# A two-block fp32 network whose residual stream is kept by token, not by channel

## The chip, the cores and the metric

One core of a Trainium2 chip runs the whole program. The metric is the device time of one execution in microseconds (us). The engines named below are TensorE (PE, matrix products; PEld is its weight load), VectorE (DVE), ScalarE (ACT), GpSimd (POOL) and SyncE (SP, which here only starts transfers).

## What is computed

A sequence of 256 tokens with 2048 channels goes through two blocks. In block 1 the residual stream h takes up a mixer (a gated recurrence beside a sparse attention), an MLP of width 8192 with a squared ReLU, and a gate fed by an embedding p of each layer. In block 2 it takes up a second mixer, a SwiGLU FFN of width 5632, a state-space mixer (s5) and another FFN. Around each part stand norms:

```python
def rms_norm(x, g):
    xf = x.astype(jnp.float32)
    y = xf * lax.rsqrt(jnp.mean(xf * xf, axis=-1, keepdims=True) + NORM_EPS)
    return (y * g.astype(jnp.float32)).astype(x.dtype)
...
h = h + rms_norm(part(rms_norm(h, gain_pre)), gain_post)
```

The last line is the pattern of a part, in short form; in the gate it is `h = h + sigmoid(h @ W_gate) * (p @ W_proj)` without norms. All of it is fp32.

## The kernel before, in words

Products are made from rounded halves: an operand x is split into x_hi (rounded, made by ACT, L245 or L248) and x_lo (the rest, made by DVE, L246 or L249); a weight chunk that was loaded as wr is split into wh (ACT, L261) and wl (DVE, L262). Each product of a weight tile is then three passes of PE: wh with x_hi and x_lo, and wl with x_hi. A chunk holds two k (a k is 128 channels of the contraction) by 512 columns, and four chunks of wh and wl are held, so that the next wh can be written once PE has ended a chunk.

`group` (L304) leaves its result by channel (128 channels on the partitions, 256 tokens along the row); `atok` (L786 to L788) leaves it by token (128 tokens on the partitions, two halves c, columns along the row). The output products of a part use `outs`, which is `atok` over column groups of 512 and, at the very end, two of 256.

h is a tile of 16 k by 256 tokens, by channel, and so is the operand X of the next product. The output Y of a part is by token, where the norm's factor r is a number for each partition. `post_norm` turns and scales at once: for each k and token half it multiplies Y by a 128x128 diagonal matrix `dg` of r on PE (L577, fp32, which the records show as two), and DVE adds the result with the gain (a number for each channel, thus for each partition) to h (L578). `make_x` calls this `upd(k)` ahead of the split of each k, so the first column group of a part runs as: update k, split k, multiply by k. Sums of squares of h, for the next norm, are one ACT square and two products with a column of ones for each k (`h_norm`, L540 and L542); r itself comes from an integer guess and three Newton steps in small DVE operations (`rsqrt_small`, L402 to L410). For s5 the squares are summed by products with a matrix of ones (L1862).

```python
        dg = [self.s([P, P], tag="dg", bufs=2) for _ in range(2)]
        for c in range(2):
            V.tensor_scalar(dg[c], self.ident, r[:, c:c + 1], None, op0=ALU.mult)
...
            for c in range(2):
                nc.tensor.matmul(pt[:, c * P:(c + 1) * P], Y[:, c, k * P:(k + 1) * P], dg[c], start=True, stop=True)
            V.scalar_tensor_tensor(self.h[:, k], pt, self.vec(gain[0], gain[1] + k), self.h[:, k], op0=ALU.mult, op1=ALU.add)
```

Each engine runs its own queue in order; a scheduler lays the queues out by priorities while the program is built. Weight loads, and what else is loaded on SP, are issued in the order of SP's queue as their buffers come free. The seams between parts are, in order: the start, mixer to MLP, MLP to gate, gate to mixer 2, mixer 2 to the first FFN, FFN to s5, s5 to the second FFN, and the end.

## Time and profile before

| | us |
|---|---|
| median of three runs (3611.12 to 3624.04) | 3619.83 |
| the profiled execution | 3617.48 |
| its span | 3615.7 |
| PE busy in it | 3485.3 |
| DVE busy | 2152.0 |
| ACT busy | 1737.1 |
| POOL busy | 904.5 |

The granted clock of PE had a mean of 0.983 of its full rate. PE is busy nearly all the time, so what matters is read from the chain that ended last: where PE's own instructions follow each other it is PE's work that sets the time, and where another engine stands in the chain PE waits for it. A busy time of PE counts overlapping instructions whole; the chain counts only what each adds.

### The profile page before, as it was taken

The page shows a single profiled execution, that of the slowest core. Times are in us where ns is not written, and L with a number is a line of the kernel's source. Part 1 is how long each engine was busy: PE and PEld are TensorE (multiplying, and loading weights), DVE is VectorE, ACT ScalarE, POOL GpSimd, SP SyncE. Part 2 cuts the span into 40 slices and gives each one's busy share as a digit, 9 for nine tenths or more (in the row PEclk, how much of TensorE's full clock was granted, in tenths as well). Part 3 has the DMA queues.
Part 4 walks back from the last instruction along what each step waited for, and adds up shares of the span by engine and source line. Part 5 has one row for each costly group of instructions (what it writes and reads, how often), then busy time and mean ns, then how long its engine had stood idle before and what let it go on. Part 6 is the DMA issues. An engine that isn't in the chain of part 4 may idle for free.

```text
span 3615.7 us, 55161 instructions
## 1 busy us (share of the span) xinstructions
PE 3485.3 (96%) x20610; PEld 2998.3 (83%) x20610; DVE 2152.0 (60%) x3323; ACT 1737.1 (48%) x2621; POOL 904.5 (25%) x1378
## 2 busy tenths in 40 slices
PE   9989999998999999999899999999779999999999
PEld 9877788886888898998788888888668888888887
DVE  6687674555555656555666466565664565465565
ACT  4656554643344554445444444344454454444443
POOL 0231022288610002010436565644310000000000
PEclk9999999998999999999999999999989999999999
DMA  7735456676776564565567777778876466665664
GB/s 218 225 111 158 135 166 195 186 217 195 218 210 198 154 198 134 147 181 181 162 207 227 235 231 220 247 217 256 284 223 195 137 187 192 192 191 188 192 189 138
DMA packets 506148, 699.28 MB, mean 193 GB/s; under 512 B 43318, under 2 KB 317143, under 8 KB 505880
## 3 DMA queue, kind: packets, MB, share of 16 engines
q1 hardware_dynamic: 473712, 628.99, 57.1%
q0 software_dynamic: 27456, 63.65, 5.8%
q8 instruction: 161, 2.64, 0.3%
q10 hardware_dynamic: 4712, 3.13, 0.3%
q14 instruction: 107, 0.88, 0.1%
HBM read 654.17 MB, written 37.22 MB: 191 GB/s over the span
## 4 chain that ended last, share of the span: by engine, by line
PE 85%; POOL 5%; DVE 4%; DMA 3%; ACT 2%; issue 1%; SPq 0%; ACTq 0%; DVEq 0%; POOLq 0%
PE ps L304 34%; PE px L304 11%; PE ps L786 11%; PE ps L788 11%; PE ps L787 11%; POOL m L1737 1%; POOL m L1738 1%; POOL m L1739 1%; PE px L577 1%; PE pm L1756 1%; DMA TBd<-m 1%; DVE wl L262 1%; ACT wh L261 1%; PE pm L542 0%; DMA m<-in_wg_dram 0%
## 5 line engine op out<-in xcount | busy, mean ns | idle before, releaser
L262 DVE TENSOR_TENSOR wl<-wr,wh 128x1024 fp32r<-128x1024 f32 x1126 | 1427.9, 1269 | 1239.7 <-ACT wh L261 1199.1
L261 ACT ACTIVATE wh<-wr 128x1024 fp32r<-128x1024 f32 x1126 | 1190.4, 1058 | 1441.0 <-PE ps L788 538.4
L304 PE MATMUL ps<-x,wh 128*128 128x512 f32 (+1 forms) x4864 | 1285.9, 353 | 12.8 <-DVE e L381 4.6
L304 PE MATMUL ps<-x,wl 128*128 128x256 f32 x3840 | 856.5, 283 | 1.5 <-DVE wl L262 1.5
L304 PEld LDWEIGHTS ps<-x,wl 128*128 128x128 f32 x3840 | 729.5, 191 | 130.3 <-issue 5.5
L304 PEld LDWEIGHTS ps<-x,wh 128*128 128x128 f32 x4864 | 760.8, 192 | 29.0 <-issue 10.8
L786 PE MATMUL ps<-wh,x 128*128 128x512 f32 (+1 forms) x2032 | 768.4, 378 | 5.6 <-ACT wh L261 3.6
L787 PE MATMUL ps<-wl,x 128*128 128x512 f32 (+1 forms) x2032 | 762.7, 375 | 0.8 <-DVE wl L262 0.8
L788 PE MATMUL ps<-wh,x 128*128 128x512 f32 (+1 forms) x2032 | 762.3, 375 | 0.0
L786 PEld LDWEIGHTS ps<-wh,x 128*128 128x128 f32 x2032 | 383.1, 189 | 79.5 <-ACT wh L261 4.1
L788 PEld LDWEIGHTS ps<-wh,x 128*128 128x128 f32 x2032 | 383.1, 189 | 70.3 <-issue 2.0
L787 PEld LDWEIGHTS ps<-wl,x 128*128 128x128 f32 x2032 | 383.5, 189 | 69.0 <-issue 1.8
L304 PE MATMUL px<-x,wh 128*128 128x512 f32 x1280 | 404.9, 397 | 1.8 <-DVE e L381 1.8
L304 PEld LDWEIGHTS px<-x,wl 128*128 128x128 f32 x1280 | 240.1, 188 | 56.7 <-issue 0.8
L304 PE MATMUL px<-x,wl 128*128 128x256 f32 x1280 | 256.0, 280 | 0.3 <-DVE wl L262 0.3
L304 PEld LDWEIGHTS px<-x,wh 128*128 128x128 f32 x1280 | 196.7, 189 | 4.7 <-issue 2.0
L245 ACT ACTIVATE x<-e 128x256 fp32r<-128x256 f32 x168 | 68.3, 411 | 87.9 <-DVE e L1540 48.7
L1798 POOL TENSOR_TENSOR m<-m,m 128x128 f32<-128x128 f32 x128 | 68.7, 559 | 120.7 <-PE pm L1756 106.7
L577 PE MATMUL px<-dg,x 128*128 128x128 f32 x384 | 62.8, 309 | 29.7 <-DVE dg L568 28.7
L246 DVE TENSOR_TENSOR x<-e,x 128x256 fp32r<-128x256 f32 x168 | 79.3, 480 | 15.4 <-ACT x L245 12.5
L1815 POOL TENSOR_TENSOR m<-m,m 128x256 f32<-128x256 f32 x64 | 59.5, 933 | 102.2 <-DMA m<-in_s5bT_dram 102.2
L577 PEld LDWEIGHTS px<-dg,x 128*128 128x128 f32 x384 | 56.6, 216 | 33.7 <-DVE dg L568 21.0
(487 smaller groups left out, 2774.2 us busy)
## 6 DMA issues: line engine op xcount, KB each, us to landing
wr<-in_w_ffn_in_dram SPq DMA_DIRECT2D x704, 256.0 KB, 3.2
wr<-in_mlp_w_dram SPq DMA_DIRECT2D x256, 512.0 KB, 4.5
wr<-in_w_ffn_out_dram SPq DMA_DIRECT2D x176, 512.0 KB, 4.8
wr<-in_w_in_dram SPq DMA_DIRECT2D x152, 512.0 KB, 3.9
wr<-in_w_out_dram SPq DMA_DIRECT2D x64, 512.0 KB, 4.0
wr<-in_w_glu_dram SPq DMA_DIRECT2D x128, 256.0 KB, 3.1
wr<-in_ple_gate_dram SPq DMA_DIRECT2D x32, 512.0 KB, 4.7
wr<-in_w_in_dram SPq DMA_DIRECT2D x32, 256.0 KB, 5.8
```

Source lines behind the costliest of these rows:

```text
L245: a = nc.scalar.activation(dst[:, 0], src, AF.Copy)
L246: b = (eng or nc.vector).tensor_tensor(dst[:, 1], src, dst[:, 0].bitcast(F32), op=ALU.subtract)
L261: nc.scalar.activation(wh, wr, AF.Copy)
L262: nc.vector.tensor_tensor(wl, wr, wh.bitcast(F32), op=ALU.subtract)
L304: mm = lambda o, w, x, a, z: nc.tensor.matmul(o, w, x, start=a, stop=z, skip_group_check=True)
L577: nc.tensor.matmul(pt[:, c * P:(c + 1) * P], Y[:, c, k * P:(k + 1) * P], dg[c], start=True, stop=True)
L786: nc.tensor.matmul(ps, xh, wh, start=first, stop=False, skip_group_check=True)
L787: nc.tensor.matmul(ps, xh, wl, start=False, stop=False, skip_group_check=True)
L788: nc.tensor.matmul(ps, xl, wh, start=False, stop=last, skip_group_check=True)
L1737: G_.tensor_tensor(o, x[:, :, 0:n], c0, op=ALU.mult)
L1798: G_.tensor_tensor(t1[:, q], u_(1), l_(1), op=ALU.mult)
L1815: G_.tensor_tensor(ob[:, :, ri], v4(gb[0][:, 0]), v4(gb[1][:, ri]), op=ALU.mult)
```

## The change

h is kept by token, as Y is. The update is then a DVE operation with r as a number for each partition (`scalar_tensor_tensor`, for two k at once and each token half, in line L603 of the changed kernel), and PE turns each 128x128 tile of h with the identity into PSUM (`tile_T`, L591), from where ACT and DVE split it (L250 and L251 there). The gain is now a number for each column, so it is loaded, spread over the partitions, into a tile `G` with one buffer by a transfer on SP (`gains`), and Y is multiplied with it ahead of the norm's factor (`settle`, L1216). Squares are summed along rows by ACT (L568). For all norms behind a part but that of s5, r comes from Ln and Exp on ACT with one Newton step in place of three; the table that these need is loaded in `outs`. x is loaded twice, by channel for the first operand and by token as h, the second behind the eighth weight load. The gate and the projection of p are computed by token with `atok`, and the second mixer, whose operand was h itself before, now has h turned. At the end the result is turned and copied out by ACT and DVE in turn. The recurrence of the first mixer has five buffers `l` where it had seven, and one stage of background work has another priority.

```diff
-        return self.e("l", bufs=7)
+        return self.e("l", bufs=5)
...
+            self.log_exp()
...
+    def rsqrt_tok(self, ss, n, tag="rt", by=None, tables=False):
...
+        if tables:
+            y = self.s([P, 16], tag="ny")[:, :2]
+            S.activation(y, ss, AF.Ln, scale=1.0 / n, bias=self.eps)
+            S.activation(y, y, AF.Exp, scale=-0.5)
+            t, u = self.s([P, 16], tag="nt")[:, :2], self.s([P, 16], tag="nu")[:, :2]
+            V.tensor_scalar(u, ss, 1.0 / n, EPS, op0=ALU.mult, op1=ALU.add)
+            V.tensor_tensor(t, y, y, op=ALU.mult)
+            V.scalar_tensor_tensor(t, t, -0.5, u, op0=ALU.mult, op1=ALU.mult)
+            V.scalar_tensor_tensor(rt, t, 1.5, y, op0=ALU.add, op1=ALU.mult)
...
-        self.upd = self.load_h(I["xT"], 2)
+        self.upd = self.load_xT()
...
+    def load_h(self, src):
+        self.h = h = self.newY()
+        v = src.rearrange("(c p) d -> p c d", p=P)
+        for i in range(0, D, 512):
+            self.nc.sync.dma_start(h[:, :, i:i + 512], v[:, :, i:i + 512])
...
-            if upd:
-                upd(k)
-            self.hold = self.split(self.xk(X, k), self.h[:, k], self.vec(gain[0], gain[1] + k) if gain else None)
+            self.hold = self.split(self.xk(X, k), upd(k), self.vec(gain[0], gain[1] + k) if gain else None)
...
-        ps = self.ps()
-        for k in range(NK):
-            q = self.e("sq", bufs=2)
-            self.last_act = nc.scalar.activation(q, self.h[:, k], AF.Square)
+        ss = self.sums()
+        for i in range(0, D, 512):
             for c in range(2):
-                nc.tensor.matmul(ps[:, c:c + 1], q[:, c * P:(c + 1) * P], self.ones[:, 0:1], start=(k == 0 and c == 0),
-                                 stop=(k == NK - 1), skip_group_check=True)
-        rt = self.rsqrt_tok(ps[:, 0:2], D, tag)
+                self.sq_sum(ss, self.h[:, c, i:i + 512], c)
+        rt = self.rsqrt_tok(self.sum_up(ss), D, tag)
...
+    def gains(self, row, cols):
+        n = cols.stop - cols.start
+        t = self.e("G", (P, 512), bufs=1)[:, 0:n]
+        src = self.I["gain"][row:row + 1, cols]
+        self.nc.sync.dma_start(t, bass.AP(tensor=src.tensor, offset=src.offset, ap=[[0, P], [1, n]]))
+        return t
...
+    def tile_T(self, k, bank={}):
+        if k % 2 == 0:
+            bank[0] = self.ps("px")
+        pt = bank[0][:, (k % 2) * T:(k % 2 + 1) * T]
         for c in range(2):
-            V.tensor_scalar(dg[c], self.ident, r[:, c:c + 1], None, op0=ALU.mult)
-        banks = {}
+            self.nc.tensor.transpose(pt[:, c * P:(c + 1) * P], self.h[:, c, k * P:(k + 1) * P], self.ident)
+        return pt
...
+        r = self.rsqrt_tok(self.sum_up(ss), D, "rp", by, tables)
         self.gpar = 2
-        def upd(k, eng=None):
+        def upd(k):
             if k % 2 == 0:
-                banks[0] = self.ps("px")
-            pt = banks[0][:, (k % 2) * T:(k % 2 + 1) * T]
-            for c in range(2):
-                nc.tensor.matmul(pt[:, c * P:(c + 1) * P], Y[:, c, k * P:(k + 1) * P], dg[c], start=True, stop=True)
-            V.scalar_tensor_tensor(self.h[:, k], pt, self.vec(gain[0], gain[1] + k), self.h[:, k], op0=ALU.mult, op1=ALU.add)
+                for c in range(2):
+                    p = self.h[:, c, k * P:(k + 2) * P]
+                    self.nc.vector.scalar_tensor_tensor(p, Y[:, c, k * P:(k + 2) * P], r[:, c:c + 1], p,
+                                                        op0=ALU.mult, op1=ALU.add)
+            return self.tile_T(k)
...
+                self.load_h(I["x"])
...
-        ld = self.load_h(I["xT"])
-        for k in range(0, NK, 4):
-            ld(k)
-        self.upd = self.post_norm(Y, ss, ("mix_post", 0))
+        self.load_h(I["x"])
+        self.upd = self.post_norm(Y, ss)
...
+    def settle(self, y, c, ss, g):
+        self.sq_sum(ss, y, c)
+        self.nc.vector.tensor_tensor(y, y, g, op=ALU.mult)
...
-            ps = self.group(lambda k: self.xk(X, k), list(range(16)),
-                            lambda k0: self.wload([((slice(None),), self.wsrc(I["ple_gate"], k0, gi * 512))]),
-                            pre=pre if gi == 0 else None)
-            if gi == 0:
-                self.dump("h2", self.h)
-            for j in range(4):
-                k = gi * 4 + j
-                z = self.evac(ps[j])
-                s = self.e()
-                S.activation(s, z, AF.Sigmoid)
-                V.tensor_tensor(s, s, self.PJ[:, k], op=ALU.mult)
-                V.tensor_tensor(self.h[:, k], self.h[:, k], s, op=ALU.add)
+            pv = self.atok(lambda k: self.xk(X, k), list(range(16)),
+                           lambda k0: self.wload([((slice(None),), self.wsrc(I["ple_gate"], k0, gi * 512))]), 512,
+                           pre=pre if gi == 0 else None)
+            cols = slice(gi * 512, gi * 512 + 512)
+            for c in range(2):
+                s = self.m([P, 512])
+                S.activation(s, pv[c], AF.Sigmoid)
+                V.tensor_tensor(s, s, self.PJ[:, c, cols], op=ALU.mult)
+                V.tensor_tensor(self.h[:, c, cols], self.h[:, c, cols], s, op=ALU.add)
+        self.upd = self.tile_T
...
-            self.upd(k)
+            pt = self.upd(k)
             if k % 2:
-                (nc.sync, nc.scalar)[k // 2 % 2].dma_start(ov[:, k - 1:k + 1], self.h[:, k - 1:k + 1])
+                nc.vector.tensor_copy(o[:, k], pt)
+                (nc.sync, nc.scalar)[k // 2 % 2].dma_start(ov[:, k - 1:k + 1], o[:, k - 1:k + 1])
+            else:
+                nc.scalar.activation(o[:, k], pt, AF.Copy)
...
-            with self.low(-3 * self.bg_low):
+            with self.low(-self.bg_low):
...
-        pr = self.summed = self.ps()[:, 0:T]
...
-        self.log_exp()
         for k in range(NK):
-            self.upd(k)
-            S.activation(U[:, :, k], self.h[:, k].rearrange("p (c s) -> p s c", s=8), AF.Copy,
-                         scale=self.vec("ng2", 64 + k))
-            sq = self.l()
-            if k % 4 == 2:
-                nc.gpsimd.tensor_tensor(sq, self.h[:, k], self.h[:, k], op=ALU.mult)
-            else:
-                S.activation(sq, self.h[:, k], AF.Square)
-            nc.tensor.matmul(pr, self.ones, sq, start=(k == 0), stop=(k == 15))
+            pt = self.upd(k)
+            S.activation(U[:, :, k], pt.rearrange("p (c s) -> p s c", s=8), AF.Copy, scale=self.vec("ng2", 64 + k))
...
-        self.rnorm(pr, D, rb)
+        self.h_norm(rb)
```

On DVE, at the first column group of the MLP (x with px is h before, x_4881 in the changed kernel; x_4934 and x_4899 are the operand; wl_5090 and wl_5055 are the fifth chunk), before:

```order
L578 SCALAR_TENSOR_TENSOR x_4901<-px_4944,vec,x_4901 128x256
L578 SCALAR_TENSOR_TENSOR x_4901<-px_4977,vec,x_4901 128x256
L249 SCALAR_TENSOR_TENSOR x_4934<-x_4901,vec,x_4934 128x256
L578 SCALAR_TENSOR_TENSOR x_4901<-px_4944,vec,x_4901 128x256
L249 SCALAR_TENSOR_TENSOR x_4934<-x_4901,vec,x_4934 128x256 x2
L578 SCALAR_TENSOR_TENSOR x_4901<-px_4977,vec,x_4901 128x256
L262 TENSOR_TENSOR wl_5090<-wr_5087,wh_5089 128x1024
L249 SCALAR_TENSOR_TENSOR x_4934<-x_4901,vec,x_4934 128x256
L578 SCALAR_TENSOR_TENSOR x_4901<-px_5010,vec,x_4901 128x256
L578 SCALAR_TENSOR_TENSOR x_4901<-px_5043,vec,x_4901 128x256
L249 SCALAR_TENSOR_TENSOR x_4934<-x_4901,vec,x_4934 128x256 x2
```

and now:

```order
L603 SCALAR_TENSOR_TENSOR x_4881<-x_3613,rp_4889,x_4881 128x256
L251 SCALAR_TENSOR_TENSOR x_4899<-px_4911,vec,x_4899 128x256
L603 SCALAR_TENSOR_TENSOR x_4881<-x_3613,rp_4889,x_4881 128x256 x9
L264 TENSOR_TENSOR wl_5055<-wr_5052,wh_5054 128x1024
L251 SCALAR_TENSOR_TENSOR x_4899<-px_4944,vec,x_4899 128x256
L251 SCALAR_TENSOR_TENSOR x_4899<-px_4977,vec,x_4899 128x256
```

Before, the updates (L578) were spread between the splits; now sixteen of 256 columns (L603) come early, nine of them in a row. The split of k 3, here from px_4944, stands behind the fifth wl, as the L249 behind wl_5090 did.

On DVE, at the end of the gate (m and e hold the sigmoid, x_11815 and x_11755 the projection of p, x_4901 and x_4881 h; L249 and L251 write the operand of the second mixer), before:

```order
L1215 TENSOR_TENSOR e_12914<-e_12914,x_11815 128x256
L381 TENSOR_TENSOR e_12918<-ps_12724,e_12919 128x256
L1216 TENSOR_TENSOR x_4901<-x_4901,e_12914 128x256
L249 SCALAR_TENSOR_TENSOR x_12935<-x_4901,vec,x_12935 128x256
L262 TENSOR_TENSOR wl_13084<-wr_13081,wh_13083 128x1024
L1215 TENSOR_TENSOR e_12922<-e_12922,x_11815 128x256
L381 TENSOR_TENSOR e_12926<-ps_12725,e_12927 128x256
L1216 TENSOR_TENSOR x_4901<-x_4901,e_12922 128x256
L249 SCALAR_TENSOR_TENSOR x_12935<-x_4901,vec,x_12935 128x256
```

and now:

```order
L1247 TENSOR_TENSOR m_12564<-m_12564,x_11755 128x512
L1247 TENSOR_TENSOR m_12568<-m_12568,x_11755 128x512
L1248 TENSOR_TENSOR x_4881<-x_4881,m_12564 128x512
L1248 TENSOR_TENSOR x_4881<-x_4881,m_12568 128x512
L251 SCALAR_TENSOR_TENSOR x_12572<-px_12579,vec,x_12572 128x256
L251 SCALAR_TENSOR_TENSOR x_12572<-px_12618,vec,x_12572 128x256
L264 TENSOR_TENSOR wl_12708<-wr_12705,wh_12707 128x1024
L251 SCALAR_TENSOR_TENSOR x_12572<-px_12579,vec,x_12572 128x256
L251 SCALAR_TENSOR_TENSOR x_12572<-px_12618,vec,x_12572 128x256
L264 TENSOR_TENSOR wl_12747<-wr_12744,wh_12746 128x1024
```

The splits, which stood between the gate's groups of 256 columns, all stand behind its last group of 512.

## Rows read from the trace of the kernel before

**Rows 1.** The page, parts 1 and 4: busy time by engine; the chain by engine.

```profile
PE 3485.3 (96%) x20610; PEld 2998.3 (83%) x20610; DVE 2152.0 (60%) x3323; ACT 1737.1 (48%) x2621; POOL 904.5 (25%) x1378
...
PE 85%; POOL 5%; DVE 4%; DMA 3%; ACT 2%; issue 1%; SPq 0%; ACTq 0%; DVEq 0%; POOLq 0%
```

**Rows 2.** Groups by line (busy us, mean ns | idle before, releaser), whole span.

```profile
L577 PE MATMUL px<-dg,x 128*128 128x128 f32 x384 | 62.8, 309 | 29.7 <-DVE dg L568 28.7
...
L542 PE MATMUL pm<-cst,sq 128*128 128x1 f32 x192 | 23.7, 232 | 0.0
```

**Rows 3.** The chain in order of time (start us, us, what), mixer to MLP.

```profile
437.12 3.45 PE px L577 x14
...
445.12 0.89 PE px L577 x8
446.01 0.34 PE pm L542 x4
...
472.90 0.78 PE pm L542 x8
```

**Rows 4.** The chain again, the first mixer's attention.

```profile
241.54 0.46 PE pm L1036 x4
```

**Rows 5.** Timeline of ACT and DVE, first chunks of the MLP (start us, us).

```profile
443.35 1.06 ACT L261 ACTIVATE wh<-wr 128x1024 fp32r<-128x1024 f32 x1 [1.83 <-issue]
...
444.44 1.23 DVE L262 TENSOR_TENSOR wl<-wr,wh 128x1024 fp32r<-128x1024 f32 x1 [0.20 <-ACT wh L261]
445.58 0.48 DVE L249 SCALAR_TENSOR_TENSOR x<-x,vec,x 128x256 fp32r<-128x256 f32 x1
...
447.30 0.88 DVE L249 SCALAR_TENSOR_TENSOR x<-x,vec,x 128x256 fp32r<-128x256 f32 x2 [0.45 <-ACT x L248]
```

**Rows 6.** The chain at the start: shares by line of 0 to 70, then pieces.

```profile
by line: PE ps L304 72.8%; PE px L542 10.5%; DMA cst<-in_cst_dram 6.7%; DVE wl L262 1.8%; PE px L645 1.5%; PE pm L421 1.0%; issue 0.8%; DVE nt L408 0.7%; ACT L494 0.7%; DVE nt L407 0.6%; DVE ny L410 0.6%; DVE dg L420 0.4%; DVE yi L402 0.3%;
...
46.81 0.17 DVE nv L476
...
47.01 0.18 DVE yi L402
...
50.76 0.71 PE pm L421 x4
```

**Rows 7.** The chain, MLP to gate.

```profile
1221.63 1.68 PE ps L304 x8
...
1223.52 4.18 PE ps L304 x24
...
1230.42 1.67 PE ps L304 x8
```

**Rows 8.** The chain, gate to mixer 2.

```profile
1298.49 45.48 PE ps L304 x320
```

**Rows 9.** Groups by line and shape: squares of 512 columns on ACT.

```profile
L556 ACT ACTIVATE m<-x 128x512 f32<-128x512 f32 x30 | 18.5, 617 | 0.3 <-DVE x L1119 0.3
```

**Rows 10.** The chain, mixer 2 to the first FFN.

```profile
1754.77 1.85 DVE yi L402
...
1808.31 0.35 PE pm L542 x4
...
1812.54 0.70 PE ps L304 x4
...
1817.99 0.74 PE px L304 x4
```

**Rows 11.** Line L249 on DVE, 1740 to 1830 (ns: min, median, max).

```profile
L249 DVE SCALAR_TENSOR_TENSOR x<-x,vec,x x16: 477/638/1404, 1762.8 to 1796.1; 128x256 fp32r<-128x256 f32 x16
```

**Rows 12.** The chain, FFN to s5.

```profile
2571.99 1.95 ACT x L1855 x3
...
2587.98 4.44 PE ps L1886 x71
```

**Rows 13.** The chain at the end.

```profile
3600.06 4.84 PE px L577 x20
```

More of the change, by code (lines that the diff above doesn't have):

```diff
@@ L62, in layout @@
     o["xT"] = np.ascontiguousarray(g["x"][0].T)
+    o["x"] = g["x"][0]
+    o["gain"] = np.concatenate([g["norm_mix_post"], g["norm_mlp_post"], g["norm_gains_2"].reshape(-1, D)])
     o["pT"] = np.ascontiguousarray(g["p"][0, 0].T)
@@ L503, in consts, with load_xT @@
         self.ident, self.ones, self.tri = self.cst[:, 0], self.cst[:, 1], self.cst[:, 2]
[L505 to L507 removed]
+    def load_xT(self):
+        x = self.xs([P, NK, T], F32)
+        v = self.I["xT"].rearrange("(k p) t -> p k t", p=P)
         def load(k):
[L510 to L513 removed]
+            if k % 2 == 0:
+                self.nc.sync.dma_start(x[:, k:k + 2], v[:, k:k + 2])
+            return x[:, k]
+        return load
+    def load_h(self, src):
[3 more added lines that the diff above has]
+            self.nc.sync.dma_start(h[:, :, i:i + 512], v[:, :, i:i + 512])
     def save_h(self):
[L516 to L519 removed]
+        d = self.dp.tile([T, D], F32, tag=self.nm("hd"), name=self.nm("hd"))
+        v = d.rearrange("(c p) d -> p c d", p=P)
+        for i in range(0, D, 512):
+            self.nc.gpsimd.dma_start(v[:, :, i:i + 512], self.h[:, :, i:i + 512])
         return d
@@ L549, in sums @@
     def sums(self):
-        self.ssn = 0
-        return self.s([P, 2, 9], tag="ss", bufs=2)
+        return [self.s([P, 2, 9], tag="ss", bufs=2), 0]
     def sq_sum(self, ss, y, c):
-        self.last_act = self.nc.scalar.activation(self.m([P, 512])[:, 0:y.shape[-1]], y, AF.Square, accum_out=ss[:, c, self.ssn:self.ssn + 1])
-        self.ssn += c
-    def post_norm(self, Y, ss, gain, by=None):
-        nc = self.nc
-        V = nc.vector
-        s2 = self.s([P, 2], tag="s2")
-        V.tensor_reduce(s2, ss[:, :, 0:self.ssn], axis=AX.X, op=ALU.add)
-        r = self.rsqrt_tok(s2, D, "rp", by)
-        dg = [self.s([P, P], tag="dg", bufs=2) for _ in range(2)]
+        self.last_act = self.nc.scalar.activation(self.m([P, 512])[:, 0:y.shape[-1]], y, AF.Square,
+                                                  accum_out=ss[0][:, c, ss[1]:ss[1] + 1])
@@ L1116, in block1 @@
             self.mix_end()
+            g = self.gains(0, cols)
             for c in range(2):
@@ L1167, in mlp, with add_up @@
             for cols, pv in self.outs(lambda k: self.xk(H, k), ks, W2, ch * 16, ch == 3, step):
-                self.add_up(Y, cols, pv, ch, ss if ch == 3 else None)
+                self.add_up(Y, cols, pv, ch, ss if ch == 3 else None, 1)
         self.ple_proj(0, behind)
-        self.upd = self.post_norm(Y, ss, ("mlp_post", 0), r2)
+        self.upd = self.post_norm(Y, ss, r2)
         self.ple_proj(1)
-    def add_up(self, Y, cols, pv, add, ss):
+    def add_up(self, Y, cols, pv, add, ss, row=None):
+        if ss is not None:
+            g = self.gains(row, cols)
         for c in range(2):
@@ L1194, in ple_proj @@
         for ch in range(half * 2, half * 2 + 2):
-            ps = self.group(lambda k: self.pX[k], [0, 1], lambda k0: self.wload(
-                [((slice(None),), self.wsrc(I["ple_proj"], 0, ch * 512))]), narrow=True)
-            for j in range(4):
-                self.evac(ps[j], out=self.PJ[:, ch * 4 + j])
+            pv = self.atok(lambda k: self.pX[k], [0, 1], lambda k0: self.wload(
+                [((slice(None),), self.wsrc(I["ple_proj"], 0, ch * 512))]), 512)
+            for c in range(2):
+                self.nc.scalar.activation(self.PJ[:, c, ch * 512:ch * 512 + 512], pv[c], AF.Copy)
     def ple(self):
@@ L1297, in mixer0 @@
             self.mix_end()
-            self.add_up(Y, cols, pv, True, ss)
+            self.add_up(Y, cols, pv, True, ss, 3)
         self.alt = True
-        ld = self.load_h(hd)
-        for k in range(0, NK, 4):
-            ld(k)
-        self.upd = self.post_norm(Y, ss, ("ng2", 16))
+        self.load_h(hd)
+        self.upd = self.post_norm(Y, ss)
     def agroup(self, Xk, load, rt, dst, gi):
@@ L2003, in s5 @@
                 self.dump("s5y", X[0])
+            g = self.gains(7, slice(k_ * P, k_ * P + w))
             for c in range(2):
```

46 lines of the change are left out of this document (21 added, 25 removed).

## Prediction

> **What bounds the kernel now.** The page's busy line comes first: TensorE (PE) works for 3485.3 of 3615.7 us, VectorE (DVE) for 2152.0, ScalarE (ACT) for 1737.1; the chain that ended last says the same, PE 85%, DVE 4%, ACT 2% [rows 1]. So the time moves where PE's work on the chain gets shorter, or where PE waits. The change removes PE work of two kinds, so the groups by line come next: the diagonal update L577 with 384 records, 62.8 us busy, and the sums of squares L542, of which the larger group has 192 records [rows 2], and 128 more stand in another bank. Busy times overlap with neighbours; on the chain eight records of L577 take 0.89 us, 0.11 each, and four of L542 0.34, 0.085 each [rows 3]. Six updates of 64 records and five norms of 64 are thus worth 42.6 and 27.2 us, before anything is added. A transpose with the identity, which the change puts in, is in the trace elsewhere: four in 0.46 us, 0.115 each [rows 4]. There will be 7 x 32 of them, 25.8 us.
>
> So the plain account of PE is 42.6 + 27.2 - 25.8 = 44 us less. The question is what the removed work was covering, and that is read seam by seam.
>
> **Seam by seam.** The walk goes from the profiled execution's 3617.5 us.
>
> *mixer to MLP.* Before, after the norm's DVE steps, L577 starts at 437.12 and 14 records take 3.45 us, 0.246 each, so the first product starts at 440.57 [rows 3]. After, Ln and Exp on ACT and four small DVE steps stand for a dozen; DVE steps are 0.2 us apart [rows 6], so r is there some 0.4 us sooner; two updates of 0.44 us (L249 has their form: 0.88 for 2 [rows 5]) and a few transposes follow, and the first product starts near 438.9: 1.7 us won. Then the inner loop. A slot of wh becomes free when PE ends a chunk of two k; ACT rounds the next wh (1.06), DVE forms wl behind it (1.23), and only then the split of the next odd k (0.48): 2.7 us from 443.35 to 446.06 [rows 5]. Before, PE had just enough to do there: eight L304, eight L577 (0.89) and four L542 (0.34), the last of which end at 446.35 [rows 3]. After, the products and two pairs of transposes are all that is left, 1.40 + 0.46. The odd split still stands behind wl on DVE, as the order of the changed kernel shows, so about 1.0 us of every chunk is a new wait, and a block of nine updates (9 x 0.44) ahead of the fifth wl makes the first of these about 2.2. The loop is then wh + wl + split + the odd k's products, 1.06 + 1.22 + 0.40 + 1.40 and four hand-offs, 4.2 to 4.3 us a chunk. By this walk the 128 products of the first group end at 473.2; before they end at 472.90 [rows 3] with some 2.9 us of L542 and of the next group among them. With all of L542 gone (64 x 0.085 = 5.4) the seam gains about **2 us**, not the 9 that its PE work suggests. s5 to the second FFN has the same form: **2 us**. Bounds of each: 4 won, 4 lost.
>
> *MLP to gate.* No sum of squares is removed. Before, four k take 8.79 us (1221.63 to 1230.42), of which eight and 24 L304 are 1.68 + 4.18 and 2.4 are a wait for L578, wl and L246 [rows 7]: 4.4 us a chunk. The new loop, 4.25, is nearly the same: **1 us** won, between 4 won and 5 lost.
>
> *gate to mixer 2.* Here nothing was applied to h before; its columns were split beside the gate's products, and PE ran 45.48 us without a gap into the first L542 [rows 8]. After, h must be turned as well: 32 transposes, 3.7 us. And the first split stands on DVE behind the last gate group's two products and two sums of 128x512. An ACT pass of that size takes about 0.62 (its square [rows 9]), a DVE pass of it some 0.7 (twice 128x256 in 0.88, less what is fixed). Sigmoid, four DVE passes and a split are 0.6 + 2.8 + 0.45, 3.9 us of idle PE. The loop of 4.25 a chunk then replaces a gapless 2.8 for about six chunks, 8.7 us with the transposes in it; L542 gives back 5.4. Together **7 us lost**, between 3 and 12.
>
> *mixer 2 to the first FFN.* GpSimd is busy there. L249, which reads two SBUF operands, has a median of 638 ns and a maximum of 1404 against 477 at best [rows 11]. The bulk updates read two SBUF operands as well and will be slowed like it, 16 for 16, while the splits now read PSUM. I price the 16 k at 40 us against 36: 4 lost. Won: 5.4 of L542; the stop for the norm, from 1808.31 to L304 at 1812.54, some 3.6, since the squares now follow h and not the loop; 2 at the start, where a single small DVE step took 1.85 us and half of these steps go; and 3 of the later wait up to 1817.99 [rows 10]. Sum **10 us** won, between 4 and 14.
>
> *start.* L542 has 10.5% of the chain's first 70 us, 7.35 us, and then PE waits for the norm's DVE steps from 46.81 until the broadcast at 50.76, 4 us [rows 6]. Both go; the 2 MB of h by token come behind the eighth weight chunk, and the second group's weights have time to spare. That is 11 us at 51; but the mixer behind it is partly a chain of DMA, DVE and GpSimd, with five instead of seven buffers for the recurrence. I take **9 us**, between 4 and 13.
>
> *FFN to s5.* Before, 64 L577 and 32 L1862 alternate with L578, the scalings and squares on ACT, and the first product behind them starts at 2587.98 [rows 12]. After, ACT is the longest: 16 scalings at 0.65 (three in 1.95 [rows 12]) and 8 squares at 0.6, 15.3 us from about 2563, then reduction, 13 small steps, broadcast and two passes, to about 2584. **4 us** won, between 0 and 5.
>
> *finish.* L577 is cold: 20 in 4.84 us [rows 13]. After, 16 updates and 8 copies on DVE, some 10 us, set the end, 2 to 3 earlier: **2 us**, between 0 and 4.
>
> **Sum.** 2 + 2 + 1 - 7 + 10 + 9 + 4 + 2 = 23 us less. On the median, 3619.8 - 23 = **3597 us**. All best ends together would be 3575, all worst 3637. The products with the gain (128x256 and 128x512 on DVE), the extra table loads on ACT and the loads of the gains on SP I cost at nothing: in the output products that cover them PE is the one that does not wait. If that cover is gone and a gain lands late, the reduction behind its product moves with it, a microsecond or so at five seams.
>
> **Rivals.** (1) *The plain account holds*: the odd splits find room, the loop is PE's own, and 40 us or more are won, 3580 or less. For it: DVE is busy only 60%. Against it: the 2.7 us are a queue, not a load [rows 5]. (2) *The waits take it all back*: the loop costs 0.3 to 0.6 us a chunk more than I walk (each split, square or update that happens to stand ahead of wh does it), and 40 chunks at five seams eat 12 to 24 of the 23: within 11 us of before, 3609 to 3631. (3) *Slower*: wh itself falls behind. On ACT each wh has one or two splits ahead of it, and in three chunks 512-wide squares that wait for updates. If wh starts 1.0 us after its slot is free, 40 chunks cost 40 us more, and the kernel comes to about 3637; it is slower than 3631 from 0.85 us a chunk on. Against it: before, wh started at 443.35, with the chunk's end [rows 5]. (4) *The clock falls*: after the idle stretch ahead of 437.12 the records ran at half rate, 0.246 [rows 3], the lower of the two levels (1.2 GHz). If new waits and the transposes between them keep it there, 32 transposes at 0.23 and a part of the products at half rate cost 5 us or more at each of five seams: 3620 to 3630. Against it: after each wait of 2.4 us the records are near the full rate, 8 in 1.68, then 24 in 4.18 [rows 7].
>
> The Trainium skill (TensorE: Matmul & The Clock Gate, Part 4: PE-mode transpose) speaks for rival 4: it says that transposes do not count as activity for the faster clock, and gives about 275 ns for one in a kernel. By it the 224 transposes would cost 61.6 us, an estimate from that page, and the change would lose; the trace has them 0.115 apart, so 275 is more likely one's latency than its spacing, and rival 4 keeps a small chance.
>
> **How the numbers follow.** My forecast (3580 to 3608) 0.52; rival 1 0.10; rival 2 0.20; rival 3 0.12; rival 4 0.06. A measurement can tell about 0.3%, 11 us, from no change. Faster is the forecast and rival 1: 0.62. Within 0.3% is rival 2 and most of rival 4: 0.25. Slower is rival 3 and the rest: 0.13. The range leaves out the lower half of rival 1 and most of rival 3: 3574 to 3630.
>
> **What would show it.** Right: L304 resumes near 439 (less what the start gave) after the mixer, then a chunk every 4.2 to 4.3 us with a 1 us wait for DVE's split each; no wait for the norm near 47 and 1810; a gap of about 4 us ahead of mixer 2. PE's busy time falls by more than the span. Wrong: a loop of 2.9 to 3.5 us a chunk (rival 1), a loop of 5 us with ACT as the releaser (rival 3), records at the half rate through the seams (rival 4); or a first mixer whose end does not move although its start does.

## The result, and the profile after

The changed kernel takes 3560.24 us in the median of four runs (3559.78 to 3564.73), the kernel before 3619.64 beside it: a ratio of 0.9841 (0.9822 to 0.9861). That is 59 us less, where the prediction had 23 less (3597) and a range down to 3574. The profiled execution took 3564.73, the longest of the four, its span 3563.0: 52.7 less than the span before, and the walk below is made on these two. Each kernel has one profile, and executions of the kernel before lie between 3608.68 and 3630.23, so a figure by place is good to some microseconds, and the medians decide what a kernel is worth.

The busy line of the page after, to be held against [rows 1], and the groups of the new lines (out<-in, count | busy us, mean ns of one | idle before, releaser), which take the place of [rows 2]:

```profile
PE 3424.4 (96%) x19926; PEld 2922.6 (82%) x19926; DVE 2186.2 (61%) x3331; ACT 1729.6 (49%) x2613; POOL 907.8 (25%) x1374
```

```profile
L568 ACT ACTIVATE m<-x 128x512 f32<-128x512 f32 (+2 forms) x116 | 63.3, 547 | 22.8 <-DVE x L1207 19.2 <-DVE x L603 2.1 <-DMA x<-in_x_dram 1.1
L591 PE MATMUL px<-cst,x 128*128 128x128 f32 x224 | 53.4, 339 | 34.2 <-DVE x L603 18.9 <-issue 4.9 <-ACT x L1887 4.3
L603 DVE SCALAR_TENSOR_TENSOR x<-x,rp,x 128x256 f32<-128x256 f32 x96 | 39.7, 478 | 0.2
L1216 DVE TENSOR_TENSOR x<-x,G 128x256 f32<-128x256 f32 (+2 forms) x68 | 35.2, 550 | 6.1 <-DMA G<-in_gain_dram 5.7 <-ACT m L568 0.4
```

PE's busy time fell by 61, the span by 53. The chain of the kernel after can't be followed to its start (its pieces add up to half the span), so the two traces are laid side by side by weight chunk: the weights are loaded in the same order in both, so the n-th `wl` on DVE is taken as the same chunk, and where its start stands earlier, time has been won. By stretch (us, negative is won):

| stretch, up to the start of chunk | predicted | measured |
|---|---|---|
| start and first mixer (110) | -9 | -4.3 |
| mixer to MLP (255) | -2 | -3.7 |
| rest of the MLP (372) | 0 | **-21.7** |
| MLP to gate, the gate (405) | -1 | -5.8 |
| gate to mixer 2 (537) | +7 | +0.4 |
| mixer 2 to the first FFN (584) | -10 | -3.7 |
| rest of that FFN (797) | 0 | -5.3 |
| s5 (802) | -4 | -3.3 |
| s5 to the second FFN (884) | -2 | -5.1 |
| the end | -2 | -0.2 |
| sum | -23 | -52.7 |

Outside the two stretches that the prediction had at nothing the sum is -25.7, close to its 23, but single seams are off by up to 7 in both directions, so the closeness of the sum is in part luck. The other 27 us come from the middle of an MLP and of an FFN, where h is not touched at all.

The MLP first. Before, PE stood still there; its waits from 835 to 940 of the kernel before (line, releaser: us in total, times, longest), and its timeline (start us, us; in brackets the idle time before):

```profile
PE pm L1756 <- POOL m L1799: 13.6, 2, 10.7
```

```profile
891.39 0.63 PE L1756 MATMUL pm<-m,m 128*32 128x128 f32 x2 [10.72 <-POOL m L1799]
...
896.89 0.63 PE L1756 MATMUL pm<-m,m 128*32 128x128 f32 x2 [2.85 <-POOL m L1799]
```

L1756 is in `prod`, the products of the background work that prepares s5 while the MLP runs. Their operands come from GpSimd, whose last step, L1799, ends at 891.3. The chain of the kernel before runs through them there, from a transfer on (start us, us, what):

```profile
865.50 11.72 DMA m<-in_s5cb_dram
878.42 1.59 POOL m L1784 x2
880.44 1.56 POOL m L1737
890.12 1.22 POOL m L1799
```

The MLP's products stand behind L1756 in PE's queue, and they did not pass it: PE is idle until it runs. Stretches of 20 us (us, then busy us and count of PE, PEld, DVE, ACT, POOL; clock, DMA share, GB/s), first of the kernel before, then of the one after:

```profile
880.00:900.00 20.00, 6.43 (x19) 2.65 (x17) 4.16 (x6) 1.21 (x4) 19.56 (x36) 0.61 0.42 134
900.00:920.00 20.00, 20.00 (x92) 15.69 (x92) 9.24 (x12) 6.87 (x10) 13.24 (x21) 0.79 0.56 167
```

```profile
880.00:900.00 20.00, 20.00 (x114) 15.77 (x112) 15.71 (x20) 10.08 (x15) 17.67 (x22) 1.00 0.82 267
900.00:920.00 20.00, 20.00 (x89) 16.33 (x89) 10.35 (x13) 8.20 (x10) 13.62 (x25) 1.00 0.64 204
```

Before, PE works for 6.43 of the 20 us from 880, and its granted clock is 0.61 there and 0.79 in the 20 us behind. After, there is no wait in these 40 us. Over the whole stretch PE has the same 1756 records in both kernels; before, they take 340.1 us and PE is idle for 14.7, after, 331.9 and 1.1. So some 13.6 us of what this stretch won are idle time, and some 8 are the same work done faster, without the lower clock. What moved is one number of the diff, `self.low(-3 * self.bg_low)` to `self.low(-self.bg_low)`: the scheduler no longer puts these products so far ahead that they reach the head of PE's queue before GpSimd has made their operands. The view of that line (who waited for what, PE and PEld added up) says so for the whole span, first before, then after:

```profile
its engine sat idle before it (us, times) until:
  POOL m L1799: 28.2, 5
```

```profile
its engine sat idle before it (us, times) until:
  issue: 13.1, 52
who waited for it (us, times):
  POOL m L1833: 164.4, 10
```

GpSimd waited for these products before too (106.7 us for L1756); after, it waits longer (164.4 us), and PE no longer waits for it.

Now the seams. PE at the first group of the MLP in the kernel after, to be held against [rows 3]:

```profile
432.24 1.67 PE L591 MATMUL px<-cst,x 128*128 128x128 f32 x4 [4.87 <-DVE x L603]
434.22 0.69 PE L591 MATMUL px<-cst,x 128*128 128x128 f32 x2 [0.32 <-DVE x L251]
434.56 1.20 PE L306 MATMUL ps<-x,wh 128*128 128x512 f32 x2
...
446.29 0.73 PE L306 MATMUL ps<-x,wh 128*128 128x512 f32 x2 [1.07 <-DVE x L251]
...
450.53 0.73 PE L306 MATMUL ps<-x,wh 128*128 128x512 f32 x2 [0.71 <-DVE x L251]
...
454.76 0.73 PE L306 MATMUL ps<-x,wh 128*128 128x512 f32 x2 [0.71 <-DVE x L251]
...
459.04 0.73 PE L306 MATMUL ps<-x,wh 128*128 128x512 f32 x2 [0.76 <-DVE x L251]
```

and ACT and DVE in one turn of that loop, the counterpart of [rows 5]:

```profile
447.76 1.06 ACT L263 ACTIVATE wh<-wr 128x1024 fp32r<-128x1024 f32 x1 [2.03 <-PE ps L306]
```

```profile
448.85 1.23 DVE L264 TENSOR_TENSOR wl<-wr,wh 128x1024 fp32r<-128x1024 f32 x1 [1.37 <-ACT wh L263]
449.99 0.87 DVE L251 SCALAR_TENSOR_TENSOR x<-px,vec,x 128x256 fp32r<-128x256 f32 x2
```

The product waits for the split L251, which stands behind wl, which waits for wh, which waits for PE to end a chunk. Three turns from 446.29 take 12.75 us, 4.25 each. This is the loop of the prediction, at its price.

### The profile page after: what moved, and what is told of

The parts are those of the page before. It is cut to its first block, busy times and chain, and to the rows that moved or that the text cites. A ratio compares the mean times of both kernels' runs of the same rounds, so it can differ in the third digit from the quotient of the medians.

```text
span 3563.0 us, 53866 instructions
## 1 busy us (share of the span) xinstructions
PE 3424.4 (96%) x19926; PEld 2922.6 (82%) x19926; DVE 2186.2 (61%) x3331; ACT 1729.6 (49%) x2613; POOL 907.8 (25%) x1374
## 4 chain that ended last, share of the span: by engine, by line
PE 46%; DVE 2%; DMA 1%; issue 1%; ACT 1%; SPq 0%; ACTq 0%; DVEq 0%
PE ps L306 18%; PE px L306 8%; PE ps L814 6%; PE ps L815 6%; PE ps L816 6%; PE pm L1791 1%; PE px L591 0%; DVE wl L264 0%; DMA wr<-in_w_ffn_in_dram 0%; ACT wh L263 0%; DMA G<-in_gain_dram 0%; PE ps L1911 0%; DMA wr<-in_w_ffn_out_dram 0%; PE pm L1923 0%; PE px L1911 0%
## 5 line engine op out<-in xcount | busy, mean ns | idle before, releaser
L306 PE MATMUL ps<-x,wh 128*128 128x512 f32 (+1 forms) x4672 | 1224.3, 352 | 33.7 <-DVE x L251 17.0
L814 PE MATMUL ps<-wh,x 128*128 128x512 f32 (+1 forms) x2160 | 819.6, 380 | 2.8 <-ACT x L247 1.6
L815 PE MATMUL ps<-wl,x 128*128 128x512 f32 (+1 forms) x2160 | 813.6, 377 | 1.3 <-DVE wl L264 1.3
L306 PE MATMUL ps<-x,wl 128*128 128x256 f32 x3648 | 813.3, 282 | 1.5 <-DVE wl L264 1.5
L816 PE MATMUL ps<-wh,x 128*128 128x512 f32 (+1 forms) x2160 | 812.7, 377 | 0.0
L306 PEld LDWEIGHTS ps<-x,wl 128*128 128x128 f32 x3648 | 692.9, 191 | 120.8 <-DVE wl L264 3.3
L306 PEld LDWEIGHTS ps<-x,wh 128*128 128x128 f32 x4672 | 731.4, 192 | 50.8 <-DVE x L251 21.8
L814 PEld LDWEIGHTS ps<-wh,x 128*128 128x128 f32 x2160 | 407.5, 189 | 84.1 <-ACT x L247 4.7
L816 PEld LDWEIGHTS ps<-wh,x 128*128 128x128 f32 x2160 | 407.2, 189 | 75.6 <-issue 2.2
L815 PEld LDWEIGHTS ps<-wl,x 128*128 128x128 f32 x2160 | 407.8, 189 | 74.0 <-issue 1.6
L1833 POOL TENSOR_TENSOR m<-m,m 128x128 f32<-128x128 f32 x128 | 71.2, 576 | 165.8 <-PE pm L1791 164.4
L591 PE MATMUL px<-cst,x 128*128 128x128 f32 x224 | 53.4, 339 | 34.2 <-DVE x L603 18.9
L1832 POOL TENSOR_TENSOR m<-m,m 128x128 f32<-128x128 f32 x128 | 78.9, 639 | 0.6
```

The source lines that it names most:

```text
L306: mm = lambda o, w, x, a, z: nc.tensor.matmul(o, w, x, start=a, stop=z, skip_group_check=True)
L591: self.nc.tensor.transpose(pt[:, c * P:(c + 1) * P], self.h[:, c, k * P:(k + 1) * P], self.ident)
L814: nc.tensor.matmul(ps, xh, wh, start=first, stop=False, skip_group_check=True)
L815: nc.tensor.matmul(ps, xh, wl, start=False, stop=False, skip_group_check=True)
L816: nc.tensor.matmul(ps, xl, wh, start=False, stop=last, skip_group_check=True)
L1832: G_.tensor_tensor(cx[:, q], u_(0), l_(0), op=ALU.mult)
```

## The experiments

Each is compared with the kernel before, run beside it; a ratio is its time over that kernel's, with a 95% interval, and "stretch" means the table's.

**Is it the number?** Theory A: the priority number of the background products makes what the prediction lacked. Rival B: they move with the rest of the change. Two kernels, the change with the old number, and the kernel before with the new one:

```
e1_prio3 (on the kernel after)
-            with self.low(-self.bg_low):
+            with self.low(-3 * self.bg_low):
e2_prio1 (on the kernel before)
-            with self.low(-3 * self.bg_low):
+            with self.low(-self.bg_low):
```

> The changed kernel with one number set back: the products of the s5 background work (prod) again have the priority of before, three times bg_low ahead, where the change has it once. Theory A (the 21.7 us that the MLP became shorter between its chunks 255 and 272, and about 4 us ahead of the s5 seam, come from this number alone: the products no longer stand in PE's queue ahead of operands that GpSimd has not made): 3560 + 22 to 26 us = 3580 to 3588, with PE waiting for GpSimd near 880 again. Rival B (they come from the rest of the change, which moved GpSimd's work and its transfers against PE): no change, 3555 to 3565.

> The kernel before with that one number of the change: the products of the s5 background work at once bg_low ahead. Theory A (the number alone): 3620 - 22 to 26 = 3594 to 3598, and no PE gap of 10.7 us near 891. Rival B (it takes the rest of the change): 3612 to 3625. Were both part of it, something between.

With the old number the changed kernel takes 3579.31 us (3576.52 to 3590.54), 0.9889 (0.9873 to 0.9906): 17 to 19 us more than with the new one (by ratios or medians), and its timeline of PE has the stall again:

```profile
883.44 0.63 PE L1791 MATMUL pm<-m,m 128*32 128x128 f32 x2 [8.68 <-POOL m L1834]
888.94 0.63 PE L1791 MATMUL pm<-m,m 128*32 128x128 f32 x2 [2.85 <-POOL m L1834]
```

In its profile 18 of the 21.7 us won in the MLP are lost again, and 2 of the 5.3 in the first FFN. The median lies just under the range of theory A. The kernel before with the new number takes 3594.17 (3584.82 to 3604.26), 0.9934 (0.9913 to 0.9955), 28 us less than the 3622.33 beside it (24 by the ratio); in the profiles -19.6 in the MLP and -5.4 in the first FFN, the two stretches that the prediction had at nothing. Theory A holds from both sides: the number is worth 17 (by the ratios 0.9889 and 0.9841) to 28 us, without any other line of the change.

**Is the loop a matter of order?** Theory Q: the 4.25 us a chunk are a queue on DVE, the odd split behind wl, and go away when updates and splits are put ahead. Rival: they are work.

```
e4_ahead (on the kernel after)
-            self.hold = self.split(self.xk(X, k), upd(k), ...)
+            with self.low(-100):
+                self.hold = self.split(self.xk(X, k), upd(k), ...)
e9_bahead (on the kernel before: the same for `upd(k)` and the split)
```

> The changed kernel with the transposes and splits of a first operand 100 steps ahead in priority, so that in DVE's queue at the first column group of the MLP the splits of k 3 to k 9 stand ahead of the wl that they stood behind. Theory Q (the loop of 4.25 us a chunk at the seams is a queue: wh, then wl, then the odd split): the waits of 0.7 to 1.1 us a chunk go, the loop falls to PE's own 3.3 us, and the seams mixer to MLP, mixer 2 to FFN and s5 to FFN gain 4 to 6 us each, gate to mixer 2 up to 8: 3535 to 3547. Rival W (the loop is the work of DVE and ACT, not its order): within 4 us of the changed kernel, 3556 to 3564.

> The kernel before (h by channel, update by products) with the same step as e4_ahead: the updates and splits of a first operand 100 steps ahead in priority. Theory Q2 (before, PE's own products filled the wait of each chunk, 4.27 us a chunk against a queue of 4.25, so there is little to win; the change is what made room that e4_ahead then took): 3605 to 3622. Rival R (the order is worth as much without the change): 25 us or more, 3595 or less.

e4_ahead takes 3527.30 (3525.0 to 3530.74), 0.974 (0.9726 to 0.9755): 33 us better than the changed kernel, and the best of all here. Its busy line, and PE's waits from 432 to 470:

```profile
PE 3417.4 (97%) x19926; PEld 2919.5 (83%) x19926; DVE 2185.4 (62%) x3331; ACT 1725.0 (49%) x2613; POOL 911.1 (26%) x1374
```

```profile
PE px L592 <- DVE x L604: 4.9, 1, 4.9
PE px L592 <- DVE x L251: 0.3, 1, 0.3
```

The waits inside the loop are gone, and chunks follow each other at 2.7 to 2.8 us. By stretch the gain lies at the four seams with a loop (6.9, 8.0, 14.5 and 5.2 us), and in all it is 8 us more than theory Q's range allowed. PE's work is the same within 7 us; what differs is the order: the splits stand two k ahead, and wl comes behind them. On the kernel before the same order gives 3613.15 (3604.7 to 3634.67), 0.999 (0.9969 to 1.0011), nothing: there the loop had the diagonal products on PE, and PE's waits for a split were 2.8 us at mixer 2 to the first FFN, 3.0 between MLP and gate and none at mixer to MLP, so there was little to win. So the change made room at the seams, and the order as laid out gave about 33 us of it back.

**Are the transposes on the path?** Theory Q says that in the waiting loops a second transpose of each tile is hidden; rival P says that PE's work is what counts.

```
e5_twoT (on the kernel after, in tile_T)
+            for _ in range(2):
                 self.nc.tensor.transpose(pt[...], self.h[...], self.ident)
```

> The changed kernel with each transpose made twice into the same place, 224 more on PE, 0.115 us each, 25.8 us in all. Theory C (at the seams PE waits for a split, and what PE does in that wait is free, as the diagonal products were before): the waits of 0.7 to 1.1 us a chunk take in the 0.46 us of the four more transposes, so the five seams with a loop cost 0 to 2 us each, s5 and the end 2 to 4 each: 3563 to 3572. Rival P (PE's work adds up): all 25.8 us, 3586.

It takes 3591.26 (3588.74 to 3592.49), 0.9915 (0.9901 to 0.993): 31 us more than the changed kernel, more even than the work added. By the total that is the rival's, and the price of the transposes was right: PE's busy time grows by 25.0 us, 0.11 for each of the 224. By place it is not one thing. PE's gaps in the loop shrink and the turn stays the same:

```profile
PE px L592 <- DVE x L251: 2.8, 2, 2.0
PE ps L306 <- DVE x L251: 1.3, 4, 0.3
```

Four waits of 0.3 stand where 0.7 to 0.8 stood, at starts 4.24 to 4.28 us apart: in the turning loop the extra transposes are hidden. The cost is elsewhere: where the loops begin (2.0 us at once; 3.9 over the changed kernel at mixer to MLP, 5.0 at s5 to the second FFN), in the gate and gate to mixer 2 (some 6), at the end (2.8), and in mixer 2 to the first FFN (7.6), where the background's products get in the way again:

```profile
PE pm L1792 <- POOL m L1835: 13.9, 1, 13.9
```

So theory C, which let a whole seam hide them, fell as well. A doubled operation measures its price at a place only if nothing else is laid out anew; here the scheduler moved the background as well.

**What were the sums worth?** The prediction counted 27.2 us of L542 on PE. In e6_nosums only the first and last k of each norm are summed on PE, so the norms lack the other fourteen (the squares are still made); e10_nosums_p1 adds the new number.

```
e6_nosums (on the kernel before, in h_norm)
+            if 0 < k < NK - 1:
+                continue
             for c in range(2):
                 nc.tensor.matmul(ps[:, c:c + 1], q[...], self.ones[:, 0:1], ...)
e10_nosums_p1: the same, and self.low(-self.bg_low) in prod
```

> The kernel before without the column-of-ones products L542 for k 1 to 14 (the sums of squares then hold k 0 and k 15 alone); the squares on ACT and all else stay. It prices the sums by themselves. Theory N (the sums of squares are what the change wins at the seams; the update by products was a cover and wins nothing): 280 of 320 records go, 24 us at 0.085 each; with the waits around them (a chunk beside them took 6 to 14 us longer at three seams) 25 to 40 us: 3580 to 3595. Rival U (the seams' gain of about 31 us is half the update's): 15 us or less, 3605 or more.

> The kernel before without L542 for k 1 to 14 (as in e6_nosums) and with the background products at once bg_low ahead (as in e2_prio1). If the two parts add (26 to 28 for the priority, some 42 for the sums where the background stall is left out), 3620 - 68 = 3552, 3547 to 3558, which is below the changed kernel: then the update by token and its transposes cost about 8 us net as they stand. If they overlap (both only remove the one stall in the MLP): 3565 or more.

e6_nosums takes 3571.58 (3570.46 to 3576.61), 0.9876 (0.9858 to 0.9893); e10_nosums_p1 3554.39 (3549.2 to 3558.82), 0.9818 (0.98 to 0.9836). By stretch, in the profiles, against the kernel before (us):

| stretch | sums left out | sums out, new number | changed kernel | changed, e4_ahead |
|---|---|---|---|---|
| start and mixer | -10.6 | -3.9 | -4.3 | -3.7 |
| mixer to MLP | -5.9 | -5.7 | -3.7 | -10.6 |
| rest of the MLP | -5.4 | -21.8 | -21.7 | -21.8 |
| MLP to gate, gate | +1.7 | +1.4 | -5.8 | -7.8 |
| gate to mixer 2 | -8.9 | -8.8 | +0.4 | -7.6 |
| mixer 2 to FFN | -9.0 | -11.3 | -3.7 | -18.2 |
| rest of the FFN | -2.1 | -4.6 | -5.3 | -4.1 |
| s5 | -0.6 | +2.2 | -3.3 | -2.4 |
| s5 to second FFN | -6.2 | -7.5 | -5.1 | -10.3 |
| sum | -47.0 | -60.0 | -52.5 | -86.5 |

Leaving out seven eighths of the sums, 280 of 320 records, is worth 47 us in the profile, 42 without what came back in the MLP's stall, where their spacing in the chain makes it 23.8. The pair with the new number (e10_nosums_p1 against e2_prio1) gives 40 in the medians. At the four seams with a loop the two pairs agree, 30.0 and 29.7 us for 224 records, and most of it is PE's own work: its busy time falls there by 26.4 and 28.2 us, 0.12 a record where the prediction had 0.085. At the start they don't agree (10.6 and 0.5), so the sum over all places is less sure. With the number the sums reach -60, more than the whole change (-52.7), and the number's part in this pair is 17 us by the medians. The rest of the change, updates and transposes, thus cost some 6 to 8 us net with the order as laid out (the intervals of the two ratios overlap): against e10_nosums_p1 it has some 26 us less of PE's work and 33 more in which PE is idle. In e4_ahead's order it gains 27; what that order does without the sums was not run.

**The small parts.** Gains and their loads left out (the result then lacks the gains); no tables, with three Newton steps everywhere; five buffers `l` in the kernel before; seven in the changed one, in the room of G, so without gains:

```
e7_nogain (on after)     -  self.nc.vector.tensor_tensor(y, y, g, op=ALU.mult)   and the DMA in gains
e8_notables (on after)   -  if tables:                    +  if False:           (no log_exp in outs)
e3_l5 (on before)        -  return self.e("l", bufs=7)    +  return self.e("l", bufs=5)
e11_nogain_l7 (on e7)    -  return self.e("l", bufs=5)    +  return self.e("l", bufs=7)
```

> The changed kernel without the products of Y and the gain, and without the gains' loads on SP (the update then adds without its gain). I had costed both at nothing. At the s5 seam the chain names a load of G of 8.8 us and a product behind it. Theory F (they are covered): 3557 to 3563. Rival G (a late gain holds back the reduction behind its product at some seams): 3 to 8 us less, 3552 to 3557.

> The changed kernel with the norm's factor from the integer guess and three Newton steps everywhere, as before, and without the table loads in the output products. By my walk Ln and Exp save about 0.4 us at each of five seams (seven DVE steps at 0.2 less two ACT passes and their hand-offs), and the table loads cost nothing: 2 us slower, 3562. Rival: the loads of 1.28 us on ACT stand ahead of a wh that PE waits for, and the kernel is 2 to 6 us faster without them, 3554 to 3558.

> The kernel before with five buffers l in place of seven, as in the change. At the start the change was 11 us ahead, behind the first mixer only 4.3. Theory L (fewer buffers hold up the recurrence): 4 to 8 us slower, 3624 to 3628, with the loss between 180 and 310 us. Rival M (the mixer's end is set by other transfers and by GpSimd, and takes an early start in): 3616 to 3623.

> The changed kernel without the products with the gain, its loads and its tile (as e7_nogain, whose median was 3556.1), and with seven buffers l in the room that this leaves. Theory L (the first mixer ends near 411.6 whatever the start, because five buffers hold up the recurrence; without sums but with seven it ended at 405.3): the mixer ends 5 to 7 us earlier than in e7_nogain, 3549 to 3551. Rival M (other things set it): within 2 us of e7_nogain, and the mixer ends near 411.

Without gains 3556.14 (3551.62 to 3560.24), 0.9828 (0.9811 to 0.9846), 4 us less than the changed kernel, with intervals that overlap; in the profile the difference is all in mixer 2 to FFN (-9.0), elsewhere at most a microsecond a stretch. But e8_notables, which has the gains, shows the same -9.1 there, so the runs don't lay it to them. Without tables 3562.30 (3561.34 to 3563.33), 0.9846 (0.983 to 0.9861), 2 more: the Ln and Exp are worth next to nothing. Five `l` in the kernel before: 3625.83 (3605.13 to 3629.73), 0.9999 (0.9981 to 1.0018), though the first mixer of its profile ends 6.9 us later. Seven in the changed kernel: 3562.06 (3560.01 to 3563.47), 0.9839 (0.9824 to 0.9854), 6 *more* than e7_nogain (by the ratios 4, within the intervals), with its mixer ending 6.2 later. More buffers did not bring the start's gain back; that theory fell.

**Both at once.** e4_ahead with seven `l`, room for them made by eight instead of nine buffers `m`, which the background uses too:

```
e12_ahead_l7 (on e4_ahead)
-        self.mp = pool("mp", 9)              +        self.mp = pool("mp", 8)
-        return self.e("l", bufs=5)           +        return self.e("l", bufs=7)
```

> e4_ahead (3527.3) with seven buffers l, for which the pool m has eight buffers in place of nine. Theory L: the mixer ends 5 to 7 us earlier, 3520 to 3523. Rival: the eighth buffer less in the background work costs as much or more, 3527 or above.

3565.39 (3562.04 to 3565.74), 0.9847 (0.9832 to 0.9861): 38 us worse than e4_ahead. The mixer ends 9 later, 10 are lost in the MLP, where PE waits for the background once more,

```profile
PE pm L1792 <- POOL m L1835: 5.1, 1, 5.1
```

and 16 between mixer 2 and the end of the first FFN. Which of the two buffer counts does it was not told apart.

## Why the prediction was wrong, step by step

**The step that failed** is one that it never took: the number of `prod`, 17 to 28 us, was put at nothing. The prediction went seam by seam and had the stretches between seams at nothing; the one line of the diff between seams, the priority of `prod`, was in the diff but in no term. The wait it feeds was in the trace of before, 13.6 us of PE and the lower clock behind it, and so was the chain through GpSimd; POOL's 5% of it stand in [rows 1]. The prediction named PE, DVE and ACT out of that row and passed over the 5%. With 17 to 28 us for that number its own sum of 23 comes to 40 to 51, against 52.7 in the profiles and 59 in the medians. The time itself falls where rival 1 had it (3580 or less), but not by rival 1's mechanism.

**The plan of the rest** was right in kind: 44 us less work on PE, of which waits at the seams take back a part. Outside the two stretches PE's busy time fell by 51.2 us and its idle time grew by 25.5. That the prediction's 23 is so near to 25.7 is in part luck, since single terms missed in both directions, as follows.

**A chain step is not a wait.** Three of its gains, 4 us near 47, 3.6 from 1808.31 and 3 up to 1817.99, were read off steps of DVE in the chain and taken for waits of PE. PE worked through them on the products behind. These are all its waits before, from 0 to 80, and then from 1797 to 1830:

```profile
PE px L542 <- DMA cst<-in_cst_dram: 6.1, 1, 6.1
PE pm L421 <- DVE dg L420: 0.2, 1, 0.2
```

```profile
PE px L304 <- DVE wl L262: 0.3, 1, 0.3
PE pm L421 <- DVE dg L420: 0.2, 1, 0.2
```

The 6.1 us are the start itself, ahead of the first product. So terms of 10.6 us had 0.7 us of idle time behind them.

**The loop** was right in kind and size: 4.25 us a turn where 4.2 to 4.3 stood, releaser DVE, waits of 0.7 to 1.1. The first product came at 434.56, 6.0 before the 440.57 of [rows 3], of which 4.3 are the earlier mixer and 1.7 the seam, as the walk had it. e4_ahead shows the mechanism: with the splits first the waits go and the turn is 2.8. So rival 1, that the splits find room, fell by the order laid out: in another they do find it.

**The sums L542** were under-sized. The prediction let them count for their spacing in the chain, 0.085 each, 27.2 us in all; at 0.12 each, as PE's busy time has it at the seams, they are some 38.

**Gate to mixer 2** was +7 and came out at +0.4. The gap was there, four passes of DVE and then a split, in the timelines of DVE and of PE:

```profile
1284.89 1.38 DVE L1247 TENSOR_TENSOR m<-m,x 128x512 f32<-128x512 f32 x2 [0.35 <-ACT m L1246]
1286.19 1.28 DVE L1248 TENSOR_TENSOR x<-x,m 128x512 f32<-128x512 f32 x2
1287.39 0.87 DVE L251 SCALAR_TENSOR_TENSOR x<-px,vec,x 128x256 fp32r<-128x256 f32 x2
```

```profile
1284.75 0.60 PE L591 MATMUL px<-cst,x 128*128 128x128 f32 x4
1285.96 0.50 PE L306 MATMUL ps<-x,wh 128*128 128x256 f32 x2 [0.61 <-ACT x L250]
1287.92 0.69 PE L591 MATMUL px<-cst,x 128*128 128x128 f32 x2 [1.46 <-DVE x L251]
```

but of 3.5 us from 1284.75 to 1288.26 PE waits 2.1, since transposes and the first products of mixer 2 fit in, and the sums gave back 8.9 where 5.4 was put (e6_nosums). **MLP to gate** won 5.8 instead of 1: its chunks take 3.5 us, not 4.25, and PE waits for no split of DVE there; `atok` asks for x_lo last, so a late split has two passes to come in, which is the likely reason. **Mixer 2 to FFN** won 3.7 instead of 10: 6.6 of the 10 were the waits that weren't there, and the loop has gaps like the MLP's (e4_ahead has 14.5 more). The 4 us for updates slowed beside GpSimd did not come: all 96 updates take 472 to 486 ns, and the 16 at this seam run while GpSimd does little (2.2 of the 8 us from 1721). Nor is the 3.7 sure: e7_nogain, e8_notables and e11_nogain_l7 won 12.2 to 12.8 in this stretch, e1_prio3 9.2, and 5.5 us of waits for DVE's `e` (L384) in the changed kernel's profile are at most 0.4 in theirs. Whether that is this one execution or the layout is open. **s5 to second FFN** won 5.1 instead of 2; without the sums alone it won 6.2. The **finish** won 0.2 instead of 2: the transposes run there at the half rate, at a granted clock of 0.54,

```profile
3549.43 1.12 PE L591 MATMUL px<-cst,x 128*128 128x128 f32 x4 [0.47 <-ACT x L1261]
```

four in 1.12, each four waiting for the copies of the four before.

**Start and mixer** won 4.3, not 9. The L542 are gone, the 4 us near 47 were none, and PE meets the weights in the place of the sums, in the timelines of PE and ACT:

```profile
56.36 0.50 PE L306 MATMUL ps<-x,wh 128*128 128x256 f32 x2 [1.41 <-ACT wh L263]
```

```profile
55.26 1.06 ACT L263 ACTIVATE wh<-wr 128x1024 fp32r<-128x1024 f32 x1 [4.95 <-DMA wr<-in_w_in_dram]
```

By chunk 40 of the mixer 6.4 is left, at its end 4.3. Between kernels whose mixer is the same code or nearly so, its end moved from 10.6 earlier (e6_nosums) to 6.9 later (e3_l5). Buffers `l` do not explain it, and each figure is of one execution, while the ten of e3_l5 lie 25 us apart; what sets it stays open.

**The clock** (rival 4). The transposes do not hold it down where products stand between them: from 434 to 466 the granted clock has a mean of 0.94, from 466 on 1.00, and the second of two transposes adds 0.11 us (two of them take 0.38, one 0.27), so the change did not lose by them. The Trainium skill (TensorE: Matmul & The Clock Gate, Part 4: PE-mode transpose) says that they do not count as work for the clock and gives about 275 ns for one. Here the duration of one record is 0.273 us in the median from 434 to 466, which agrees, but they follow each other faster. Only where nothing but transposes runs, at the end, is the clock near its lower level (0.54, where 1.2 GHz is 0.5), which would agree with the Trainium skill, but waits stand beside them, so that this trace can't say whose doing it is.

## What to carry to other kernels

Read every line of a diff against the wait that it feeds, the plain numbers too: where an in-order queue serves a main loop and a background, the priority of the background decides whether the loop stands behind an operand that isn't there, and the trace names that wait by its line. Price the work that is taken off an engine by what its busy time loses in a run without it: the spacing in the chain had 0.085 for a sum that cost 0.12. Before a step of another engine in the chain is called a wait, look whether the first engine stood still there. When work goes, the next queue, here a split behind a weight's rounding, takes part of the gain back until the order is changed as well. So after a change that frees an engine, look for the new wait in the loop, see what stands ahead of its releaser, and move that: it was worth 33 us here, more than half of the change.

## What the runs showed that was not expected

A stall of 13.6 us cost more than 20: the granted clock was 0.61 in the 20 us around it and 0.79 in the 20 us behind, and the same records took 8 us longer. And a kernel with such a background is sensitive to things that should not matter: one buffer fewer of one kind and two more of another cost 38 us, a second transpose, with which GpSimd has nothing to do, brought a wait of 13.9 us for GpSimd, and the first mixer's end moved by 17 us between the profiles of kernels with nearly the same mixer.
